# The RWKV scan of a hybrid diffusion backbone: its small products on 64-row tiles, without zero-padded operands

## The chip, the cores and the metric

One core of a Trainium2 chip runs the whole forward pass in one launch. The metric is device time in microseconds, the median of several runs. The engines are called as the profile calls them: PE is TensorE's matmuls, PEld its weight loads, DVE VectorE, ACT ScalarE, POOL GpSimd, SP SyncE, which only issues DMAs here.

## The reference: what is computed

Two layers over 256 context and 256 latent tokens of width 1024. The even layer mixes tokens by retention and grouped-query attention and has a dense SwiGLU; the odd one mixes by differential attention and a bidirectional RWKV-7 scan and has eight experts, of which each token takes two. Only the scan, in the odd layer's mixer, is touched here. It has 8 heads of 64 features and, per head and direction, a 64 x 64 state:

```
def step(s, inp):
    rt, wt, kt, vt, at, bt = inp
    s_new = (s * wt[:, :, None, :]
             + jnp.einsum('bhvk,bhk->bhv', s, at)[..., None] * bt[:, :, None, :]
             + vt[..., None] * kt[:, :, None, :])
    y = jnp.einsum('bhvk,bhk->bhv', s if read_before else s_new, rt)
    return s_new, y
...
for d in range(2):
    f = (lambda t: t[:, ::-1]) if d else (lambda t: t)
    yc, state = rwkv_scan(*[f(t) for t in ctx_dirs[d]], zero, read_before=bool(d))
    yl, _ = rwkv_scan(*[f(t) for t in lat_dirs[d]], state, read_before=bool(d))
```

The context's tokens are scanned first, only for their state; the latent tokens' outputs `y` of both directions are added, normalized per head, scaled and gated, and multiplied with the output projection together with the attention's result.

## The kernel before

The scan runs in chunks of 64 tokens: a half (half 0 is the context, half 1 the latent tokens) has four chunks, and both directions `d` walk them, one upwards, one downwards. Features lie on partitions, two heads to a group of 128: head `2 p + h` has partitions `64 h` to `64 h + 63` of group `p`. `prep` leaves per direction and half the decayed operands `AR` (a and r) and `BK` (b and k), and the chunk decay `WC`. Inside a chunk a unit triangular system is solved; its inverses come ahead of the scan from `inv_blocks` (32 x 32 blocks by TensorE), `inv_diag` (forward substitution, columns shared by VectorE, `tmv`, and GpSimd, `tmg`, both updating `N`) and `inv_join` (`X`, transposed by VectorE, then products `gp` and `wp`), and are stored in `XF`.

`step` handles one chunk of one direction, in four parts between yields:

- the operands: `lm` = products of `BK` with the a and r columns, masked on VectorE into `Lm` (L1128); `bkt` and the lower half of `UV` by transposes (L1132, L1139);
- `z` = `Lm` x `UV` (L1149) plus, from the second chunk on, a x the state `St` (L1152), copied to `zs` (L1158);
- `u` = the inverse `XF` x `zs` (L1162), copied into the upper half of `UV` by ScalarE and VectorE (L1164, L1165);
- `s` = `bkt` x `UV` (L1172), which with `St` and `WC` gives the next state (L1179, L1180); in half 1 also the outputs `Y` (L1187, L1189).

Products of one head have only 64 rows, but are done over all 128 partitions here: the head's operand stands in a buffer whose other 64 partitions are zero. `pad` (four buffers, a and r) and `zpad` (two, for `z`) are cleared by GpSimd once per chain (L1103); their halves are copied in by VectorE and ScalarE (L1118, L1158).

```
pd = pad[cnt[0] % 4]
for h in range(2):
    hs = slice(64 * h, 64 * h + 64)
    (S.copy if h else V.tensor_copy)(pd[hs, :, h, 0:w], ar[hs, :, c])
```

`chain(half)` sends both directions through their steps and prepares the next chunk's operands behind `z`. `chain(0)` is emitted side by side with the second half's `inv_diag` and `inv_join`, `chain(1)` with `finish`, which prepares the gate (`G1`, `G2`) and weights (`whi`, `wlo`) of the output projection. `Y` has two PSUM banks, one per block of 128 tokens. Behind the scan each block is normalized, transposed (L478) and multiplied (`mms`, L267 to L269); `moe_open` lets SP send the experts' weights (L1411), whose buffers take the scan's place in memory.

The code says what depends on what; the order of the instructions on each engine is set by the framework's scheduler when the kernel is built, and stays so, on SP's queue of DMAs too. An fp32 product shows as two records in the profile.

## Time and profile before

| | |
|---|---|
| Time, median of 3 runs | 2155.31 us (2152.7 to 2157.81) |
| Profiled execution, span | 2153.4 us; the page gives no other time of it |
| Busy: PE, PEld | 2045.5 us (95%), 1635.4 us (76%) |
| Busy: DVE, ACT, POOL | 1663.8 (77%), 1220.2 (57%), 166.0 us (8%) |
| DMA | 493.99 MB, mean 229 GB/s |
| Granted TensorE clock, mean | 0.976 |

Busy shares are means over stages with different limits. The page's picture of the span in 40 slices, each 53.8 us, shows this: the DMA engines are busy nine tenths from slice 22 on, where the experts' weights stream in, and nearly idle in slices 17 to 20, where the scan runs. In a row the array's tile stands as rows x columns (128\*64), and a record's duration is longer than the distance to the next record's start, since matmuls are pipelined; distances between starts tell the rate.

### The profile page before, as it was taken

The page shows a single profiled execution, that of the slowest core. Times are in us where ns is not written, and L with a number is a line of the kernel's source. Part 1 is how long each engine was busy: PE and PEld are TensorE (multiplying, and loading weights), DVE is VectorE, ACT ScalarE, POOL GpSimd, SP SyncE. Part 2 cuts the span into 40 slices and gives each one's busy share as a digit, 9 for nine tenths or more (in the row PEclk, how much of TensorE's full clock was granted, in tenths as well). Part 3 has the DMA queues.
Part 4 walks back from the last instruction along what each step waited for, and adds up shares of the span by engine and source line. Part 5 has one row for each costly group of instructions (what it writes and reads, how often), then busy time and mean ns, then how long its engine had stood idle before and what let it go on. Part 6 is the DMA issues. An engine that isn't in the chain of part 4 may idle for free. (4 is left out here: it accounts for less than half of the span.)

```text
span 2153.4 us, 30029 instructions
## 1 busy us (share of the span) xinstructions
PE 2045.5 (95%) x11521; PEld 1635.4 (76%) x11522; DVE 1663.8 (77%) x2099; ACT 1220.2 (57%) x1581; POOL 166.0 (8%) x223
## 2 busy tenths in 40 slices
PE   6999989999999999858999999999999999999997
PEld 2767778777887766748887888888888787888875
DVE  3977783674557556688568999889989999899987
ACT  3543342222235445633337777777777777777775
POOL 0211110000000110284001000000000000000000
PEclk8999999999999999969999999999999999999999
DMA  8435351475645331101077999999999999999993
GB/s 297 160 109 168 110 172 55 152 244 187 203 150 166 111 88 45 36 16 51 21 268 258 366 317 350 332 347 367 355 343 352 350 372 347 339 352 357 366 353 144
DMA packets 224202, 493.99 MB, mean 229 GB/s; under 512 B 11355, under 2 KB 45262, under 8 KB 224054
## 3 DMA queue, kind: packets, MB, share of 16 engines
q1 hardware_dynamic: 219968, 482.62, 64.4%
q10 hardware_dynamic: 4086, 9.40, 1.3%
q8 instruction: 92, 1.51, 0.3%
q14 instruction: 56, 0.46, 0.1%
HBM read 490.87 MB, written 1.11 MB: 228 GB/s over the span
## 5 line engine op out<-in xcount | busy, mean ns | idle before, releaser
L273 DVE TENSOR_TENSOR mlo<-mraw,mhi 128x1024 fp32r<-128x1024 f32 x668 | 789.1, 1221 | 79.2 <-ACT mhi L272 62.4
L272 ACT ACTIVATE mhi<-mraw 128x1024 fp32r<-128x1024 f32 x668 | 682.9, 1057 | 104.3 <-PE y L269 49.0
L262 ACT ACTIVATE whi<-raw 128x1024 fp32r<-128x1024 f32 (+1 forms) x150 | 153.0, 1024 | 279.6 <-PE acc L269 109.6
L263 DVE TENSOR_TENSOR wlo<-raw,whi 128x1024 fp32r<-128x1024 f32 (+1 forms) x146 | 175.1, 1203 | 137.8 <-ACT whi L262 137.4
L267 PE MATMUL acc<-hTh,whi 128*128 128x512 f32 (+1 forms) x504 | 190.7, 380 | 0.0
L268 PE MATMUL acc<-hTl,whi 128*128 128x512 f32 (+1 forms) x504 | 186.6, 371 | 0.0
L269 PE MATMUL acc<-hTh,wlo 128*128 128x512 f32 (+1 forms) x504 | 185.6, 369 | 0.0
L268 PE MATMUL g<-mlo,xh 128*128 128x512 f32 x448 | 182.5, 407 | 0.3 <-POOL mlo L1581 0.3
L337 DVE SCALAR_TENSOR_TENSOR part<-mraw,cond,part 128x1024 f32<-128x1024 f32 x112 | 147.8, 1341 | 40.3 <-DMA mraw<-in_mod_w 40.2
L267 PE MATMUL g<-mhi,xh 128*128 128x512 f32 x448 | 178.6, 399 | 0.0
L267 PE MATMUL u<-mhi,xh 128*128 128x512 f32 x448 | 177.3, 396 | 0.0
L268 PE MATMUL u<-mlo,xh 128*128 128x512 f32 x448 | 177.3, 396 | 0.0
L269 PE MATMUL u<-mhi,xl 128*128 128x512 f32 x448 | 177.1, 395 | 0.0
L269 PE MATMUL g<-mhi,xl 128*128 128x512 f32 x448 | 177.1, 395 | 0.0
L268 PE MATMUL y<-mlo,acts 128*128 128x512 f32 x448 | 175.7, 392 | 0.3 <-DVE mlo L273 0.3
L269 PE MATMUL y<-mhi,acts 128*128 128x512 f32 x448 | 174.8, 390 | 0.0
L267 PE MATMUL y<-mhi,acts 128*128 128x512 f32 x448 | 151.4, 390 | 0.0
L267 PE MATMUL acc<-whi,hTh 128*128 128x512 f32 x336 | 137.7, 413 | 5.3 <-ACT whi L262 3.4
L268 PE MATMUL acc<-wlo,hTh 128*128 128x512 f32 x336 | 135.8, 404 | 4.5 <-DVE wlo L263 4.5
L269 PE MATMUL acc<-whi,hTl 128*128 128x512 f32 x336 | 134.7, 402 | 0.0
L267 PEld LDWEIGHTS acc<-hTh,whi 128*128 128x128 f32 x504 | 95.3, 190 | 22.4 <-issue 4.1
L268 PEld LDWEIGHTS acc<-hTl,whi 128*128 128x128 f32 x504 | 95.0, 189 | 17.6 <-issue 2.8
(437 smaller groups left out, 3510.1 us busy)
## 6 DMA issues: line engine op xcount, KB each, us to landing
mraw<-in_moe_w_gate SPq DMA_DIRECT2D x112, 1024.0 KB
mraw<-in_moe_w_up SPq DMA_DIRECT2D x112, 1024.0 KB
mraw<-in_moe_w_down SPq DMA_DIRECT2D x110, 1024.0 KB
mraw<-in_mod_w SPq DMA_DIRECT2D x96, 512.0 KB
raw<-in_ffn_w_down SPq DMA_DIRECT2D x32, 512.0 KB
raw<-in_odd_w_in SPq DMA_DIRECT2D x26, 512.0 KB
raw<-in_even_w_in SPq DMA_DIRECT2D x24, 512.0 KB
raw<-in_ffn_w_gate SPq DMA_DIRECT2D x20, 512.0 KB
```

The source lines that it names most:

```text
L262: S.activation(h, v, AF.Copy)
L263: (eng or V).tensor_tensor(l, v, h, op=ALU.subtract)
L267: T.matmul(out, ah, bh, start=first, stop=False)
L268: T.matmul(out, ah, bl, start=False, stop=False)
L269: T.matmul(out, al, bh, start=False, stop=last)
L272: S.activation(hi, src, AF.Copy)
L273: eng.tensor_tensor(lo, src, hi, op=ALU.subtract)
L337: V.scalar_tensor_tensor(part[r], w, c_, part[r], op0=ALU.mult, op1=ALU.add)
```

## The change

The zero-padded buffers, their clearing and their copies are gone. Products of one head take the 64 partitions they need, on a 64-row tile of the array (`tile_position=(64 * h, ...)`), and loops go over the heads so that neighbours have different parity `h`. `lm`, `u` and `Y` have a PSUM bank per parity; `Y`'s banks no longer stand for blocks of tokens, so the normalization goes by parity too, and the transposes wait for both. Masked evictions of `Lm` in half 0 are two of half the size. `zs` is one copy, VectorE's for one direction and ScalarE's for the other. The steps of a chain are emitted in a new order: `z` of both directions, operands of the next chunk for direction 0, `u` of both, operands for direction 1, `s` of both, then all outputs.

```diff
-        pad, zpad = [], []
         def chain_pool():
-            e, q = top_pool("chain")
-            pad[:] = [q.tile([128, 4, 2, 128], F32, name=f"pad{i}") for i in range(4)]
-            zpad[:] = [q.tile([128, 4, 2, 64], F32, name=f"zpad{i}") for i in range(2)]
-            for t in pad + zpad:
-                G.memset(t, 0.0)
-            return e, q
+            return top_pool("chain")
+        heads = [(p, h, slice(64 * h, 64 * h + 64)) for p in range(4) for h in range(2)]
...
+        def prepare(d, half, c):
+            a = [acc("lm") for h in range(2)]
+            for p, h, hs in heads:
+                T.matmul(a[h][:, p * w:(p + 1) * w], bk[hs, p, c].rearrange("p a t -> p (a t)"), ar[hs, p, c, 0:w],
+                         start=True, stop=True, tile_position=(64 * h, 0))
             for h in range(2):
-                hs = slice(64 * h, 64 * h + 64)
-                (S.copy if h else V.tensor_copy)(pd[hs, :, h, 0:w], ar[hs, :, c])
...
+                V.tensor_tensor(Lm[:, 4 * h:4 * h + 4, 0:w], a[h][:, 0:4 * w].rearrange("p (a t) -> p a t", a=4),
+                                rc(f"rmask{d}")[:, None, 0:w].to_broadcast([128, 4, w]), op=ALU.mult)
...
+        def state_in(d):
+            for p, h, hs in heads:
+                hd = 2 * p + h
+                T.matmul(zv[hs, p], Lm[:, 4 * h + p, 0:64], UV[:, hd * 64:hd * 64 + 64], start=(p == 0),
+                         stop=(S0 is None and p == 3), tile_position=(0, 64 * h), skip_group_check=True)
+            if S0 is not None:
+                for p, h, hs in heads:
+                    T.matmul(zv[hs, p], ar[hs, p, c, 0:64], S0[hs, p], start=False, stop=(p == 3),
+                             tile_position=(64 * h, 64 * h), skip_group_check=True)
+            zs[d] = q.tile([128, 4, 64], F32, name="zs", tag="zs", bufs=2)
+            (S.copy if d else V.tensor_copy)(zs[d], zv)
+
+        def solve(d, half):
+            u = [acc("u") for h in range(2)]
+            for p, h, hs in heads:
+                T.matmul(u[h][0:64, p * 64:p * 64 + 64], XF[half][hs, d, c, p], zs[d][hs, p],
+                         start=True, stop=True, tile_position=(64 * h, 0))
...
+        def state_out(d, half):
+            for p, h, hs in heads:
+                hd = slice((2 * p + h) * 64, (2 * p + h) * 64 + 64)
+                T.matmul(sv_[hs, p], bkt[:, hd], UV[:, hd], start=True, stop=True, tile_position=(0, 64 * h))
...
+        def outputs(was, states, i):
+            for part in range(2):
+                for p, h, hs in heads:
+                    for d in range(2):
+                        o_, at_ = 64 * (c % 2), (c // 2) * 256 + p * 64
+                        dst = Y[h][o_:o_ + 64, at_:at_ + 64]
+                        if part == 0:
+                            T.matmul(dst, Lm[:, 4 * h + p, 64:128], UV[:, hd], start=(i == 0 and p == 0), stop=False,
+                                     tile_position=(0, o_), skip_group_check=True)
+                        else:
+                            T.matmul(dst, ar[hs, p, c, 64:128], states[d][hs, p], start=False,
+                                     stop=(i == 3 and p == 3), tile_position=(64 * h, o_), skip_group_check=True)
...
         def chain(half):
+            for i in range(4):
+                for d in range(2):
+                    state_in(d)
+                yield
...
+                ahead(0)
+                for d in range(2):
+                    solve(d, half)
+                yield
+                ahead(1)
+                for d in range(2):
+                    state_out(d, half)
+                yield
+                if half:
+                    outputs(was, states, i)
...
-            V.tensor_tensor(yc, yc, G1[:, b], op=ALU.mult)
-            V.tensor_tensor(yc, yc, G2[:, b], op=ALU.add)
-            split_to(mh[:, 4:8, b * 128:b * 128 + 128], ml[:, 4:8, b * 128:b * 128 + 128], tr4(yc))
+            V.tensor_tensor(ycb, ycb, parity(G1, h), op=ALU.mult)
+            V.tensor_tensor(parity(yf, h), ycb, parity(G2, h), op=ALU.add)
+        for b in range(2):
+            split_to(mh[:, 4:8, b * 128:b * 128 + 128], ml[:, 4:8, b * 128:b * 128 + 128], tr4(yf[:, b]))
```

How the instructions move, in three places. First TensorE in the second chain, where a step's `z` ends and the next step's operands begin (numbers behind names tell buffers and PSUM tiles apart); before:

```order
L1149 MATMUL z_8712<-UV_8685,Lm_8669 64x64
L1152 MATMUL z_8712<-St_8426,pad1_8628 64x64
L1126 MATMUL lm_8734<-pad2_8629,BK01_6852 128x256 x2
L1126 MATMUL lm_8738<-pad2_8629,BK01_6852 128x256 x2
L1132 MATMUL tp_8742<-cst_all_64,BK01_6852 128x128 x4
L1139 MATMUL tp_8751<-cst_all_64,vT_5386 128x128 x4
```

and in the changed kernel:

```order
L1137 MATMUL z_8713<-UV_8677,Lm_8657 64x64 x8
L1141 MATMUL z_8713<-St_8442,AR01_6851 64x64 x8
L1137 MATMUL z_8732<-UV_8705,Lm_8685 64x64 x8
L1141 MATMUL z_8732<-St_8454,AR11_6854 64x64 x8
L1244 MATMUL tp_8751<-cst_all_64,vT_5386 128x128 x4
L1111 MATMUL lm_8760<-AR01_6851,BK01_6852 128x128
L1111 MATMUL lm_8761<-AR01_6851,BK01_6852 128x128
```

The two kinds of `z` products, which took turns, now stand in eights; `lm` has twice as many products, of 128 columns and not 256, which alternate between two banks.

Then VectorE at the start of the scan, with the last columns of the first inversion (`tmv`, `N`); before:

```order
L1037 TENSOR_TENSOR tmv<-M,N 128x14
L1039 TENSOR_TENSOR N<-N,tmv 128x7x2
L1118 COPY pad_7760<-AR_6334 64x4x64
L1037 TENSOR_TENSOR tmv<-M,N 128x12
L1039 TENSOR_TENSOR N<-N,tmv 128x6x2
```

and in the changed kernel:

```order
L1037 TENSOR_TENSOR tmv_7345<-M_7064,N_7084 128x14
L1114 TENSOR_TENSOR Lm_7788<-lm_7790,cst_rwkv_5376 128x4x64
L1039 TENSOR_TENSOR N_7084<-N_7084,tmv_7345 128x7x2
L1114 TENSOR_TENSOR Lm_7847<-lm_7848,cst_rwkv_5376 128x4x64
L1037 TENSOR_TENSOR tmv_7351<-M_7064,N_7084 128x12
```

The pad copies are gone from between the columns (five stood before the transposes `X`), and five half evictions of `Lm` stand there, where one whole one stood.

Last VectorE behind the scan, where `yc` is the normalized output (G1 and G2 scale, gate and shift it); before, up to the first block's split into `mixl`:

```order
L1276 TENSOR_TENSOR yc_9367<-yc_9367,G2_8600 128x512
L1274 TENSOR_TENSOR yc_9390<-yc_9390,yrs_9396 128x512
L263 TENSOR_TENSOR wlo_9474<-raw_8610,whi_9473 128x1024
L273 TENSOR_TENSOR mixl_8598<-tp_9380,mixh_8597 128x4x128
L1275 TENSOR_TENSOR yc_9390<-yc_9390,G1_8599 128x512
```

and in the changed kernel, up to both blocks' splits:

```order
L1282 TENSOR_TENSOR yc_9424<-yc_9424,yrs_9430 128x512
L1283 TENSOR_TENSOR yc_9424<-yc_9424,G1_8627 128x512
L1284 TENSOR_TENSOR yf_9404<-yc_9424,G2_8628 128x8x64
L263 TENSOR_TENSOR wlo_9547<-raw_8642,whi_9546 128x1024
L273 TENSOR_TENSOR mixl_8626<-tp_9437,mixh_8625 128x4x128
L273 TENSOR_TENSOR mixl_8626<-tp_9444,mixh_8625 128x4x128
```

The splits now stand behind both sequences. On TensorE 48 products of the output projection stand between the scan and these transposes; before, 37 stood ahead of the first block's and 52 ahead of the second's. GpSimd's queue loses the pads' memsets (6 per chain) and is otherwise in its old order, SP's queue is unchanged.

## Rows read from the trace of the kernel before

**Rows 1.** Stages: us, busy time of each engine (x instructions), granted clock, DMA share, GB/s
```profile
961.70:1007.50 45.80, 42.66 (x774) 39.55 (x773) 39.35 (x105) 17.42 (x37) 21.36 (x52) 0.95 0.07 20
1007.50:1029.70 22.20, 17.68 (x359) 15.08 (x357) 18.55 (x26) 9.97 (x18) 8.15 (x10) 0.77 0.37 120
1029.70:1091.90 62.20, 62.11 (x886) 57.06 (x885) 29.95 (x60) 18.72 (x38) 2.97 (x4) 1.00 0.06 17
1200.00:2000.00 800.00, 800.00 (x3602) 648.80 (x3601) 720.24 (x690) 611.31 (x658) 0.00 (x0) 1.00 0.97 350
```
**Rows 2.** Time line at the scan's end, SP's queue: start, us, engine, line, op
```profile
1090.99 1.38 SPq L1411 DMA_DIRECT2D mraw<-in_moe_w_gate  x1
```
**Rows 3.** Time line at the scan's start; in brackets the idle time before, and its releaser
```profile
953.00 3.62 POOL L1103 MEMSET pad<- 128x1024 f32 x4
953.99 4.18 DVE L1118 COPY pad<-AR 64x256 f32<-64x256 f32 x1 [3.97 <-POOL pad L1103]
...
961.73 2.11 DVE L1048 STREAM_TRANSPOSE X<-N 128x1024 f32<-128x1024 f32 x1
```
**Rows 4.** VectorE by line, 970 to 1007.5 us: busy us, mean ns | idle before
```profile
L1128 DVE TENSOR_TENSOR Lm<-lm,cst_rwkv 128x512 f32<-128x512 f32 x7 | 4.8, 687 | 0.6 <-PE lm L1126 0.5
L1158 DVE COPY zpad<-z 64x256 f32<-64x256 f32 x7 | 2.9, 416 | 3.2 <-PE z L1152 3.1
...
L1118 DVE COPY pad<-AR 64x256 f32<-64x256 f32 x3 | 1.1, 367 | 0.3 <-PE z L1152 0.3
```
**Rows 5.** Time line of TensorE in the second chain, products on one tile after another
```profile
1056.24 0.60 PE L1139 MATMUL tp<-cst_all,vT 128*128 128x128 f32 x4
...
1059.44 0.28 PE L1187 MATMUL Y<-UV,Lm 128*64 128x64 f32 x2
1059.56 0.28 PE L1189 MATMUL Y<-St,pad 128*64 128x64 f32 x2
```
**Rows 6.** The same time line where two column tiles take turns
```profile
1061.19 0.22 PE L1172 MATMUL s<-UV,bkt 128*64 128x64 f32 x1
...
1061.19 0.22 PE L1189 MATMUL Y<-St,pad 128*64 128x64 f32 x1
...
1061.25 0.22 PE L1172 MATMUL s<-UV,bkt 128*64 128x64 f32 x1
```
**Rows 7.** Block products on 64-row tiles: the window's clock, then their time line
```profile
935.00:940.00 5.00, 2.91 (x166) 2.91 (x170) 5.00 (x8) 0.00 (x0) 4.77 (x4) 0.50 0.02 3
...
938.73 0.24 PE L1011 MATMUL off<-AR,BK 64*32 64x32 f32 x1
...
938.83 0.32 PE L1008 MATMUL dg<-AR,BK 64*32 64x32 f32 x6
```
**Rows 8.** Time line between the chains: transposes, pads and the first copy of z
```profile
1007.50 2.10 DVE L1048 STREAM_TRANSPOSE X<-N 128x1024 f32<-128x1024 f32 x1
...
1014.28 4.47 POOL L1103 MEMSET pad<- 128x1024 f32 x4 [20.02 <-PE s L1172]
...
1021.69 2.08 DVE L1118 COPY pad<-AR 64x512 f32<-64x512 f32 x4
...
1031.72 0.41 DVE L1158 COPY zpad<-z 64x256 f32<-64x256 f32 x1 [1.29 <-PE z L1152]
```
**Rows 9.** TensorE by line in the second chain, 1029.7 to 1091.9 us
```profile
L1187 PE MATMUL Y<-UV,Lm 128*64 128x64 f32 x128 | 15.5, 224 | 0.0
```
**Rows 10.** Time line of TensorE where `z` on 128\*64 tiles is followed by `lm`
```profile
1051.16 0.28 PE L1152 MATMUL z<-St,pad 128*64 128x64 f32 x2
1051.38 1.99 PE L1126 MATMUL lm<-pad,BK 128*128 128x256 f32 x8
```
**Rows 11.** Time line behind the scan: the two blocks' transposes, and VectorE before the second
```profile
1100.58 0.62 PE L478 MATMUL tp<-cst_all,yc 128*128 128x128 f32 x4
...
1104.51 0.68 DVE L1276 TENSOR_TENSOR yc<-yc,G 128x512 f32<-128x512 f32 x1
...
1106.66 0.60 PE L478 MATMUL tp<-cst_all,yc 128*128 128x128 f32 x4
```

More of the change, by code (lines that the diff above doesn't have):

```diff
@@ L1110, in step @@
[L1110 removed]
+        St, Y, ops, zs = {}, {}, {}, {}
+        heads = [(p, h, slice(64 * h, 64 * h + 64)) for p in range(4) for h in range(2)]
+        def prepare(d, half, c):
             bk, ar = BK[d, half], AR[d, half]
[L1112 to L1129 removed]
@@ L1145, in step @@
             zv = z[:, 0:256].rearrange("p (a v) -> p a v", a=4)
-            for h in range(2):
-                for p in range(4):
-                    hd = 2 * p + h
-                    T.matmul(zv[64 * h:64 * h + 64, p], Lm[:, hd, 0:64], UV[:, hd * 64:hd * 64 + 64],
-                             start=True, stop=S0 is None, tile_position=(0, 64 * h))
-                    if S0 is not None:
-                        T.matmul(zv[64 * h:64 * h + 64, p], pd[:, p, h, 0:64], S0[:, p],
-                                 start=False, stop=True, tile_position=(0, 64 * h))
@@ L1154, in step @@
-            zs = zpad[cnt[1] % 2]
-            cnt[1] += 1
-            for h in range(2):
-                hs = slice(64 * h, 64 * h + 64)
-                (S.copy if h else V.tensor_copy)(zs[hs, :, h], zv[hs])
-            yield
-            u = acc("u")
-            for hd in range(8):
-                T.matmul(u[0:64, hd * 64:hd * 64 + 64], XF[half][:, d, c, hd // 2], zs[:, hd // 2, hd % 2],
-                         start=True, stop=True, tile_position=(0, 0))
-            S.copy(UV[0:64, 0:256], u[0:64, 0:256])
@@ L1167, in step @@
+        def state_out(d, half):
+            c, ar, Lm, bkt, UV = ops[d]
+            S0 = St.get(d)
             s = acc("s")
             sv_ = s[:, 0:256].rearrange("p (a v) -> p a v", a=4)
[L1169 to L1173 removed]
+            for p, h, hs in heads:
+                hd = slice((2 * p + h) * 64, (2 * p + h) * 64 + 64)
+                T.matmul(sv_[hs, p], bkt[:, hd], UV[:, hd], start=True, stop=True, tile_position=(0, 64 * h))
@@ L1180, in step @@
                 V.tensor_tensor(Sn, Sn, wc, op=ALU.mult)
-            if half:
-                b, o_ = c // 2, 64 * (c % 2)
-                first = (o_, b) not in seen
-                for hd in range(8):
-                    p, h = hd // 2, hd % 2
-                    last = (o_, b) in seen and hd == 7
-                    T.matmul(Y[b][o_:o_ + 64, hd * 64:hd * 64 + 64], Lm[:, hd, 64:128], UV[:, hd * 64:hd * 64 + 64],
-                             start=(first and hd == 0), stop=False, tile_position=(0, o_), skip_group_check=True)
-                    T.matmul(Y[b][o_:o_ + 64, hd * 64:hd * 64 + 64], pd[:, p, h, 64:128], S0[:, p],
-                             start=False, stop=last, tile_position=(0, o_), skip_group_check=True)
-                seen.add((o_, b))
@@ L1195, in chain, with ahead @@
         def chain(half):
-            gens = [[step(d, half, i if d == 0 else 3 - i) for d in range(2)] for i in range(4)]
-            for g in gens[0]:
-                next(g)
+            at_ = lambda d, i: i if d == 0 else 3 - i
+            for d in range(2):
+                prepare(d, half, at_(d, 0))
             for i in range(4):
-                live = list(gens[i])
-                first_ = True
-                while live:
-                    for g in list(live):
-                        if next(g, 1) == 1:
-                            live.remove(g)
-                    if first_ and i < 3:
-                        for g in gens[i + 1]:
-                            next(g)
-                        first_ = False
-                    yield
+                for d in range(2):
+                    state_in(d)
+                yield
+                was, states = dict(ops), dict(St)
+                nxt = {}
+                def ahead(d):
+                    if i < 3:
+                        prepare(d, half, at_(d, i + 1))
+                        nxt[d] = ops[d]
+                        ops[d] = was[d]
+                ahead(0)
[3 more added lines that the diff above has]
+                ahead(1)
+                for d in range(2):
+                    state_out(d, half)
+                yield
+                if half:
+                    outputs(was, states, i)
+                ops.update(nxt)
+                yield
@@ L1254, in layer1 @@
         banks(acc=range(4), y=(4, 5))
-        for b in range(2):
-            Y[b] = ybank("Y")
+        for h in range(2):
+            Y[h] = ybank("Y")
         weave((chain(1), 16), (finish(), 10))
@@ L1262, in layer1 @@
         cur["xn"] = 2
-        for b in range(2):
-            y = Y[b]
-            yv = y.rearrange("p (h w) -> p h w", h=8)
+        yf = yp.tile([128, 2, 512], F32, name="yf")
+        parity = lambda x, h: x.rearrange("q b (p h w) -> q b p h w", p=4, h=2)[:, :, :, h]
+        for h in range(2):
+            yv = Y[h].rearrange("p (g w) -> p g w", g=8)
             m = st.tile([128, 8], F32, name="ym")
```

39 lines of the change are left out of this document (11 added, 28 removed).

## The prediction

> **What bounds the kernel now.** I read the stage table first, then the time line of the handover to the experts, then the scan's stretches by line, then single matmuls. The stage table [rows 1] shows the experts' stage, from 1200 us on, with the DMA engines at 0.97 and 350 GB/s and TensorE busy throughout: it runs at its own pace, whatever came before. Its stream of weights starts only when the scan's last products are issued: SP sends the first megabyte at 1090.99 us [rows 2]. So what the scan loses or gains moves the end of the kernel one for one, unless the few steps between scan and experts change too. The scan itself has three stretches that differ.
>
> In the last one, 1029.7 to 1091.9 us (the second half's chain, `chain(1)`), TensorE is busy 62.11 of 62.20 us at full clock, VectorE only 29.95 [rows 1]: TensorE's stream of small products is the bound. In the first, VectorE is: it idles 3.97 us for a copy into `pad0`, which waits for GpSimd's memsets of the pads (from 953.00, 3.62 us), and then that copy takes 4.18 us [rows 3] where its like take 0.37 [rows 4], so that the transposes of the block inverses start at 961.73 [rows 3]. Between them the first half's chain shares VectorE with the inversion of the second half's blocks (39.35 of 45.80 us busy [rows 1]).
>
> **The price of a small product.** An fp32 product is two records in this trace. Eight records of `Y`, four each of two products that alternate on one tile, start 0.06 us apart: the pairs stand at 1059.44 and 1059.56 [rows 5], so 58 ns a record. Where the order happens to put `Y` and `s` records of different column tiles side by side, two start together: both at 1061.19, the next at 1061.25 [rows 6]: half the price, 29 ns. On 64-row tiles the records of the block products (32 columns at the granted clock of 0.50, that is 1.2 GHz: half the columns at half the clock, so 58 ns each if alone) come six in 0.32 us where one lasts 0.24: (0.32 - 0.24) / 5 = 16 ns [rows 7]. So different tiles do work side by side, also row tiles, and the bounds for a 64-column record are 16 ns (four tiles in flight) and 58 ns (none). I take 29 ns, two tiles in flight, as the rows of the same size show it [rows 6].
>
> **The change, part by part.** All gains are against the profiled span of 2153.4 us.
>
> *A. Start of the scan.* The pads' memsets and copies go. The stop on VectorE, 3.97 + 4.18 = 8.1 us [rows 3], goes with them. Added before the transposes: five half evictions of `Lm` instead of one whole (0.69 [rows 4]); a half has 256 columns, and a copy of 256 columns takes 0.42 [rows 4], so +1.4 us, while four more pad copies of 0.37 [rows 4] go, -1.5. The products they evict now stand behind transposes at the slow clock; I put 2 us for that. GpSimd ended its own part of the inversion at 953.0, ahead of the new point. Gain 8.1 - 2 = 6 us.
>
> *B. First chain beside the inversion.* On VectorE, 970 to 1007.5 us: seven whole evictions (4.8 us) become eleven halves (4.6), seven half copies of `z` (2.9) become four whole ones (the other direction's are ScalarE's; 1.7), the pad copies (1.1) go [rows 4]: 2.5 us. Its 3.1 us of waiting for `z` I leave as it is. Gain 2.5.
>
> *C. Join and start of the second chain.* Before, from the first transpose at 1007.50 to the first copy of `z` at 1031.72 there are 24.2 us. GpSimd's second set of memsets (from 1014.28, 4.47 us) and the pad copies (1021.69, 2.08 us) stand ahead of the first `lm` product [rows 8]. Without pads these products run during the join, so at VectorE's 14.2 us mark it evicts four `Lm` (4 x 0.69) and does one weight split, about 4 us, less 1 us of pad and `z` copies inside the join: 17.5 us. Gain 6.7. The clock is at 0.77 in this stretch [rows 1]; I assume the same after.
>
> *D. Second chain.* 64-column records: `z` 256, `u` 128, `s` 128, `Y` 256 (two groups of 128, one of them in [rows 9]), 768 in all, from 58 to 29 ns: 44.2 us become 22.1. `lm`: 48 records of 256 columns at (1.99 - 0.39) / 7 = 0.23 us [rows 10], 11 us, become 96 of 128 columns on two row tiles; one alone is priced by the transposes of 128 columns, (0.60 - 0.27) / 3 = 0.11 [rows 5], two in flight 0.057: 5.5 us. Together -27.6. Against it: some records overlap already (the prices above, with 48 transposes and `finish`'s share of about 4 us, add up to 65 us in a 62.2 us window), 3 us; the order now changes the array's tiling some 24 times more, and a change costs 1051.38 - 1051.22 - 0.06 = 0.10 us [rows 10], 2.4 us; and with the work halved the chain `St` to `z` to `u` to `UV` to `s` shows in places, above all in the last step, where nothing is prepared for a next one, 2 us. VectorE's 29.95 us stay under the 42 that are left. Gain 27.6 - 7.4, about 20 us.
>
> *E. Behind the scan.* The output now needs both head parities before its transposes. Before, the first block's transposes stood behind 37 products of the output projection, at 1100.58, 8.7 us behind the chain, and the second's at 1106.66 [rows 11]. Now 48 products, at 8.7 / 37 = 0.235 us 11.3 us, stand ahead of both, and both wait for VectorE's two sequences, which ended near 1105.2, some 14 us behind. TensorE waits about 3 us, where it waited 1.5 before. Loss 1.5 us. ScalarE's table load and the weight loads on SP keep their places; SP's first load now waits for the first chain's `Lm` and not for a pad, and is freed long before its split.
>
> Sum: -6 - 2.5 - 6.7 - 20 + 1.5 = -33.7, a span of 2119.7 us. The page gives no time beside the span; the median of the runs, 2155.3, is 1.9 us more, which I add: **2121.5 us**.
>
> **A rule to weigh.** The rows show `Y` and `s` records, both over all 128 rows and on different column tiles, starting together [rows 6], and I price by that. The Trainium skill, TensorE: Matmul & The Clock Gate, section "The mechanism", says that a weight load overlaps matmuls in flight only where the row group differs. By that, neighbours that differ in columns alone would gain nothing, which is the first rival below and its 2132.5 us; the trace speaks against it in the one place it shows.
>
> **The rivals.**
> 1. *Column neighbours don't overlap.* The `Lm` half of `z`, `s` and the first half of `Y` (64 products each, 384 records) lie over all 128 rows and keep 29 ns more each, 11 us: 2132.5. Against it: [rows 6]. For it: there only a few records in a row do so.
> 2. *Row tiles don't overlap either*, or the doubled weight loads of `lm` take the gain. D is then nothing (768 x 58 ns stay, `lm` too, the tiling changes come on top, and the overlap already there covers them): -6 - 2.5 - 6.7 + 1.5 = -13.7, 2141.5. Against it: [rows 7].
> 3. *More than two tiles in flight* in `Y` and deeper interleaving (16 ns): 768 x 13 ns = 10 us more, until VectorE's 30 us and the chain's waits stop it; I allow 8: 2113.5.
> 4. *The clock falls* in the second chain, because TensorE, its work halved, waits between steps. The mean is 0.77 in the join [rows 1], and 0.50 where TensorE worked 2.91 of 5 us [rows 7]. The 42 us of work left would take 84 at 1.2 GHz, +42, so -33.7 + 42 = +8: 2163, slower. It turns to a loss once four fifths of that work run at the low level (33.7 / 42). Against it: at the low level the work itself would fill TensorE, and the window behind the join, which TensorE fills, has 1.00 [rows 1].
> 5. *The change does not do what it says*: in the first chain the scheduler puts the `lm` products of one parity together, four on one row tile. That stretch is VectorE's, so the time stays 2121.5 and it has no chance of its own; in the second chain they alternate.
>
> **How the numbers follow.** Forecast 0.60, rival 1 0.10, rival 2 0.13, rival 3 0.12, rival 4 0.05. A measurement of this kernel tells about 0.2%, 4.3 us, from no change. Of rival 4 part of the way lands within that. So faster 0.95, same 0.03, slower 0.02. The forecast's own range is 2113 to 2131 (A to C may each miss by 3 us, D by 5). The range for 8 in 10 goes from 2110 to 2142: it takes in the rivals 1 to 3 up to their own times and leaves rival 4 and the far ends out.
>
> **What would show it.** The transposes of the first inverses near 955 us, those of the second near 999; the first copy of `z` of the second chain near 1016; the first load of expert weights near 1055; in the second chain `z`, `u`, `s` and `Y` records 29 ns apart and the granted clock at 1.00; TensorE's wait behind 48 output products. A chain that still lasts 60 us would prove D wrong, a first load at 1055 with an end past 2130 the one-for-one carry, a granted clock under 0.9 there would be rival 4.

## The result, and the profile after

The changed kernel takes 2131.68 us (median of 4 runs, 2128.83 to 2133.62), the kernel before in runs beside it 2154.52: a ratio of 0.9889, 95% interval 0.9875 to 0.9903. Its profiled execution is 2132.66 us with a span of 2130.9, which is 22.5 less than before's span. The forecast was 2121.5 and a gain of 33.7: the direction and the main mechanism held, and a third of the gain did not come.

The first view is the table of stretches of the changed kernel (busy time of each engine with its instructions, granted clock, DMA share, GB/s), cut at the points that the prediction named:

```profile
948.00:957.70 9.70, 9.70 (x41) 8.03 (x41) 4.60 (x24) 2.46 (x5) 5.59 (x16) 0.50 0.27 84
957.70:1005.10 47.40, 46.61 (x811) 40.99 (x813) 35.03 (x103) 13.79 (x27) 20.99 (x52) 0.71 0.04 13
1005.10:1025.20 20.10, 18.66 (x404) 16.39 (x402) 14.24 (x23) 8.43 (x14) 1.92 (x4) 0.66 0.42 134
1025.20:1067.30 42.10, 41.64 (x901) 35.40 (x899) 25.32 (x50) 13.94 (x28) 1.97 (x4) 1.00 0.07 26
```

The second chain is 42.1 us long where it was 60.3, TensorE still fills it, and its clock is 1.00: that is the gain. But the first chain's stretch is as long as before, and its clock column reads 0.71 where before's read 0.95 [rows 1]; the join reads 0.66 where it was 0.77.

Next VectorE's time line of the changed kernel, with the idle time before an instruction and its releaser in brackets:

```profile
942.28 2.02 DVE L1018 STREAM_TRANSPOSE M<-Lc 128x1024 f32<-128x1024 f32 x1
...
952.39 0.42 DVE L1114 TENSOR_TENSOR Lm<-lm,cst_rwkv 128x256 f32<-128x256 f32 x1 [2.19 <-PE lm L1111]
...
956.57 0.42 DVE L1114 TENSOR_TENSOR Lm<-lm,cst_rwkv 128x256 f32<-128x256 f32 x1 [2.26 <-PE lm L1111]
...
957.76 2.06 DVE L1048 STREAM_TRANSPOSE X<-N 128x1024 f32<-128x1024 f32 x1
...
971.09 0.42 DVE L1114 TENSOR_TENSOR Lm<-lm,cst_rwkv 128x256 f32<-128x256 f32 x1 [4.80 <-PE lm L1111]
...
1005.10 2.05 DVE L1048 STREAM_TRANSPOSE X<-N 128x1024 f32<-128x1024 f32 x1
...
1018.86 1.29 DVE L1114 TENSOR_TENSOR Lm<-lm,cst_rwkv 128x512 f32<-128x512 f32 x2 [2.76 <-PE lm L1111]
...
1022.55 1.29 DVE L1114 TENSOR_TENSOR Lm<-lm,cst_rwkv 128x512 f32<-128x512 f32 x2 [2.41 <-PE lm L1111]
...
1025.15 0.42 DVE L1144 COPY zs<-z 128x256 f32<-128x256 f32 x1 [0.17 <-PE z L1141]
...
1067.31 1.29 DVE L1274 TENSOR_REDUCE ym<-Y 128x8 f32<-128x512 f32 x2 [0.51 <-PE Y L1186]
```

The same time line of the kernel before gives the two ends that were not shown yet:

```profile
942.38 2.02 DVE L1018 STREAM_TRANSPOSE M<-Lc 128x1024 f32<-128x1024 f32 x1
...
1091.99 1.29 DVE L1267 TENSOR_REDUCE ym<-Y 128x8 f32<-128x512 f32 x2 [0.80 <-PE Y L1189]
```

With these and [rows 3, 8] the span falls into five stretches, and each term of the sum into one of them (us):

| stretch | before | after | measured | predicted |
|---|---|---|---|---|
| transpose of `M` to the first transposes of `X` | 19.35 | 15.48 | -3.9 | A -6 |
| to the second transposes of `X` | 45.77 | 47.34 | +1.6 | B -2.5 |
| to the first copy of `z` of the second chain | 24.22 | 20.05 | -4.2 | C -6.7 |
| to the first reduction of `Y` | 60.27 | 42.16 | -18.1 | D -20 |
| to the end of the span | 1061.41 | 1063.59 | +2.2 | E +1.5 |

The bracketed waits point to one cause for A, B and C. VectorE's waits, grouped by who waited for whom (total, times, longest), from 940 us to the first copy of `z`; the first fence is the changed kernel, the second the kernel before:

```profile
DVE Lm L1114 <- PE lm L1111: 18.0, 8, 4.8
```
```profile
DVE Lm L1128 <- PE lm L1126: 3.6, 6, 1.0
```

VectorE now waits 18.0 us for `lm`, where it waited 3.6. TensorE was not idle meanwhile: in the rows above it is busy all of 948 to 957.7 us at 0.50, the 1.2 GHz level. In the kernel before, where it began later, it was at full clock from some 962.5 us on, but for a dip to 0.60 in 976 to 980 us, behind 3 us without work. Two explanations fit these rows: TensorE is late because it is slow (theory C, the clock), or because `lm` waits in its queue for something else, such as the bank that `off` holds (theory P, the place). The experiments start there.

### The profile page after: what moved, and what is told of

The parts are those of the page before. It is cut to its first block, busy times and chain, and to the rows that moved or that the text cites. A ratio compares the mean times of both kernels' runs of the same rounds, so it can differ in the third digit from the quotient of the medians.

```text
span 2130.9 us, 30220 instructions
## 1 busy us (share of the span) xinstructions
PE 2038.5 (96%) x11649; PEld 1621.1 (76%) x11650; DVE 1646.4 (77%) x2083; ACT 1210.4 (57%) x1557; POOL 152.6 (7%) x211
## 5 line engine op out<-in xcount | busy, mean ns | idle before, releaser
L267 PEld LDWEIGHTS acc<-hTh,whi 128*128 128x128 f32 x504 | 95.4, 190 | 22.5 <-issue 4.1
```

Of the source, the lines that this page charges most:

```text
L267: T.matmul(out, ah, bh, start=first, stop=False)
```

## The experiments

All times of stretches come from the profiled executions, one of each kernel. The kernels e1 to e9 are described below the table. Its columns are: transposes of `M` to first `X`; first to second `X`; second `X` to first copy of `z`; from there to the reduction of `Y`; the granted clock from 956 to 976 us; median time and ratio to before.

| kernel | M-X | X-X | X-z | z-Y | clock | time, ratio (95%) |
|---|---|---|---|---|---|---|
| before | 19.35 | 45.77 | 24.22 | 60.27 | mostly 1.00 | 2154.5 |
| changed | 15.48 | 47.34 | 20.05 | 42.16 | 0.50 | 2131.7, 0.9889 (0.9875 to 0.9903) |
| e1 same tile | 15.53 | 53.58 | 22.99 | 51.94 | 0.50 | 2148.9, 0.9981 (0.9971 to 0.9992) |
| e2 two Lo | 17.67 | 42.51 | 20.19 | 42.16 | 0.50 | 2130.0, 0.9895 (0.9881 to 0.9909) |
| e3 before, alternating | 19.36 | 41.78 | 23.49 | 54.26 | mostly 1.00 | 2143.3, 0.9957 (0.9941 to 0.9972) |
| e4 dense start | 10.68 | 40.20 | 23.44 | 42.17 | 1.00, from 968 us lower | 2126.8, 0.9875 (0.9853 to 0.9898) |
| e5 + late loads | 10.87 | 48.00 | 21.09 | 42.17 | 0.50 | 2121.8, 0.9842 (0.9828 to 0.9856) |
| e6 grouped z | 15.48 | 47.36 | 20.24 | 40.53 | 0.50 | 2130.9, 0.9890 (0.9874 to 0.9906) |
| e7 all three | 10.66 | 39.36 | 20.49 | 41.44 | 1.00, from 968 us lower | 2121.1, 0.9841 (0.9827 to 0.9855) |
| e8 + last step | 10.86 | 47.02 | 20.48 | 40.22 | 0.50 | 2121.8, 0.9832 (0.9810 to 0.9854) |
| e9 + dense join | 10.87 | 39.27 | 21.36 | 39.33 | 1.00, from 968 us lower | 2119.7, 0.9833 (0.9818 to 0.9849) |

**Does the overlap of neighbours make D?** The heads in another order, so that neighbours share a tile:

```
-heads = [(p, h, slice(64 * h, 64 * h + 64)) for p in range(4) for h in range(2)]
+heads = [(p, h, slice(64 * h, 64 * h + 64)) for h in range(2) for p in range(4)]
```

> The changed kernel with the heads taken in another order: first the four of one parity, then the four of the other, so that neighbours lie on the same tile. Tiles, operands, banks and evictions stay. Theory (the gain of the second chain is the overlap of neighbours on different tiles): of its 64-column records the 512 of z, u and s go from about 29 back to 58 ns (+14.8 us), the 128 records of the second part of Y from 15 to 29 ns (+1.8), the 96 records of lm from 59 to about 112 ns (+5.1). From the first copy of z to the first reduction of Y it takes 42.2 + 21.7, about 62 to 64 us, as before the change, and the whole kernel loses 22 to 30 us (the join and the first chain lose a little too): 2154 to 2162. Rival (the gain comes from what is no longer computed or copied: zeros, pads, two evictions instead of one): the stretch stays within 3 us of 42.2 and the time within 5 us of 2131.7.

The second chain takes 51.94 us and the kernel 17 us more than the changed kernel (less than the 22 expected). TensorE's time line of this kernel in the second chain, start and length of a run of records; the last four lines are a place where `z` ends on one tile and `u` begins on another:

```profile
1035.85 0.96 PE L1141 MATMUL z<-St,AR 64*64 64x64 f32 x16
...
1037.33 1.71 PE L1111 MATMUL lm<-AR,BK 64*128 64x128 f32 x16
...
1039.99 1.54 PE L1150 MATMUL u<-zs,XF 64*64 64x64 f32 x32
...
1082.12 0.22 PE L1141 MATMUL z<-St,AR 64*64 64x64 f32 x1
1082.17 0.22 PE L1150 MATMUL u<-zs,XF 64*64 64x64 f32 x1
1082.18 0.22 PE L1141 MATMUL z<-St,AR 64*64 64x64 f32 x1
1082.23 0.22 PE L1150 MATMUL u<-zs,XF 64*64 64x64 f32 x1
```

and that of the changed kernel:

```profile
1025.64 0.68 PE L1141 MATMUL z<-St,AR 64*64 64x64 f32 x16
1026.26 0.66 PE L1244 MATMUL tp<-cst_all,vT 128*128 128x128 f32 x4
1026.84 1.16 PE L1111 MATMUL lm<-AR,BK 64*128 64x128 f32 x16
...
1036.04 0.69 PE L1186 MATMUL Y<-St,AR 64*64 64x64 f32 x32
```

A lone 64-column record lasts 0.22 us by itself, so sixteen of `z` in 0.68 start (0.68 - 0.22) / 15 = 31 ns apart on alternating tiles, and (0.96 - 0.22) / 15 = 49 ns in this order. `lm`, with 0.28 for the last, goes from 59 to 95 ns. The 49 ns are a mean, not the pace of one tile: in the last four lines the records of each tile start 0.06 us apart, like the 58 ns of the kernel before, though these products have 64 rows, and the two tiles run side by side. Eight records on one tile are followed by eight on the other, and at each such border the last of one run beside the first of the next. That is one reason why the expectation was 10 to 12 us too high: it put 58 ns between all of them.

The new order of the heads costs 9.8 of the 18.1 us of D. The other 8.3 do not come without alternation, because this edit leaves one in place: the outputs `Y` of the two directions lie on different column tiles and still take turns, record by record. TensorE's busy time with `Y` (then its records, clock, DMA share and GB/s) in the kernel before, in e1 and in the changed kernel:

```profile
1020.00:1095.00 75.00, 16.44 (x256) 0.95 0.11 32
1020.00:1095.00 75.00, 8.63 (x256) 0.93 0.24 78
1020.00:1095.00 75.00, 6.96 (x256) 0.98 0.41 144
```

`Y` alone is 7.8 us shorter in e1 than before. So nearly all of D is tiles taking turns, about half of it by heads and most of the rest by directions; leaving out the zeros saves TensorE little by itself in this chain, since 64 rows cost the same 58 ns on one tile as 128. The stretch is not near 42.2, so the rival falls. The records that lie on four tiles, Y's state part, run (0.69 - 0.22) / 31 = 15 ns apart: the prediction's rival 3 is right for that half of `Y`.

**Columns alone.** The kernel before, with only the order of `z` and `s` changed, operands still padded:

```
-for h in range(2):
-    for p in range(4):
+for p in range(4):
+    for h in range(2):
...
-            T.matmul(zv[64 * h:64 * h + 64, p], pd[:, p, h, 0:64], S0[:, p],
+    for h in range(2):
+        if S0 is not None:
+            T.matmul(zv[64 * h:64 * h + 64, p], pd[:, p, h, 0:64], S0[:, p],
```

> The kernel before with one part of the change alone: in z and in s neighbours lie on different column tiles (the four of one pair of heads are Lm h0, Lm h1, St h0, St h1). The zero-padded operands, the 128-row products of u and lm, Y's order, the memsets and all copies stay. Theory (column neighbours overlap): 256 records of z and 128 of s in the second chain go from 58 to 29 ns, 384 x 29 = 11 us, so the stretch from the first copy of z to the first reduction of Y goes from 60.3 to about 49 us and the kernel to about 2143.5, while the transposes of X stay at 961.7 and within 2 us of 1007.5. Rival (neighbours that differ in columns alone do not overlap, and the gain in the changed kernel is that of the row tiles): the stretch stays within 2 us of 60.3, and the time is 2152 to 2156.

```profile
1038.92 0.34 PE L1149 MATMUL z<-UV,Lm 128*64 128x64 f32 x4
1039.08 0.29 PE L1153 MATMUL z<-St,pad 128*64 128x64 f32 x4
1039.20 0.29 PE L1149 MATMUL z<-UV,Lm 128*64 128x64 f32 x4
```

Four records start every 0.117 us, 29 ns apiece, though all lie over 128 rows and differ in columns alone. The time is as expected, 2143.3, but not by the expected way: the second chain gives 6.0 us and not 11, and the first chain gives 4.0 us, where two were allowed. In the second chain TensorE is busy with `z` for 7.30 us where it was 11.62, and with `s` for 6.08 where it was 7.54: before, the borders between tiles had overlapped already, and part of `s` had lain beside `Y` [rows 6]. The rival falls. The Trainium skill, TensorE: Matmul & The Clock Gate, section "The mechanism", has weight loads overlap only where the row group differs. By that these records would have stayed at 58 ns; the 29 ns measured decide against it.

**Why are A, B and C short? The bank.** Two buffers for `Lo`, so that `off`'s bank is free earlier:

```
-Lo = qI.tile([128, 16, 32], F32, name="Lo", tag="Lo", bufs=1)
+Lo = qI.tile([128, 16, 32], F32, name="Lo", tag="Lo", bufs=2)
```

> The changed kernel with two buffers instead of one for Lo, so that the bank of the off-diagonal products of the second half is freed before the first half's join and the other parity's lm of the first step need not wait for it. Theory P (the first chain is late because that bank is held): VectorE's wait of 4.80 us for lm before 971.09 us goes, the second transposes of X start near 1000.5 instead of 1005.1, and the kernel gains 4 to 5 us: 2127. Theory C (it is late because TensorE, busy without a gap from 948 to 982 us, works at a granted clock of 0.50): the lm come in another order, but the same work stands ahead, the granted clock stays at 0.50 till about 980, and the second transposes start within 2 us of 1005.1: 2130 to 2133.

The clock stays at 0.50 till 984 us, as theory C had it; but the second transposes start at 1002.22, and counted from the transposes of `M` they gain 2.6 us (1.63 + 1.55 + 0.79 + 1.69 us of waits stand ahead of the first transposes, which lose 2.2, and the wait of 4.80 is gone). The time, 0.9895, is not different from the changed kernel's 0.9889. So the truth lies between the two theories: the bank costs a part of B, since without its wait the stretch between the transposes is 4.8 us shorter, and nearly half of that is lost again in the start.

**The clock.** The first four transposes of the first chain, four times over:

```
 t = tpp()
-for p in range(4):
+for p in [p for _ in range(4 if (half, d, c) == (0, 0, 0) else 1) for p in range(4)]:
     T.transpose(t[:, p * 128:(p + 1) * 128], bk[:, p, c].rearrange("p a t -> p (a t)"), ident)
```

> The changed kernel with the first four transposes of the first chain (BK of direction 0) made four times over, so that 20 transposes of 128 rows and 128 columns follow one another at 948.5 us instead of 8. Twelve of them are of no use and cost 12 x 0.27 = 3.2 us at the low clock. Theory C (the first chain is late because TensorE works at the low clock): the granted clock rises to 1.00 near 953 instead of 984, the first transposes of X start up to 3 us later (961), but VectorE's waits for lm behind them (4.80, 1.24, 2.00 and 1.13 us) shrink to under half, and the second transposes of X start near 1001 instead of 1005.1: 2127 to 2130. Theory P (what is late is held by a bank or by VectorE, not by TensorE's speed): whatever the clock does, both transposes of X start 2 to 3 us later than in the changed kernel, and the time is 2133 to 2135.

VectorE's time line and the stretches of this kernel:

```profile
955.28 2.11 DVE L1048 STREAM_TRANSPOSE X<-N 128x1024 f32<-128x1024 f32 x1
...
995.48 2.08 DVE L1048 STREAM_TRANSPOSE X<-N 128x1024 f32<-128x1024 f32 x1
```
```profile
952.00:956.00 4.00, 4.00 (x22) 3.71 (x21) 3.48 (x17) 1.19 (x2) 3.45 (x11) 0.63 0.48 150
956.00:960.00 4.00, 4.00 (x88) 3.56 (x87) 3.99 (x5) 2.38 (x4) 3.47 (x10) 1.00 0.00 0
```

The clock rises near 955 us, and both transposes of `X` come early: the second one 9.6 us before the changed kernel's, though some 3 us of useless work stand ahead of it and the run reached the scan 2.3 us later. The longest wait for `lm` before the join is 0.20 us. Theory P falls for the stretch as a whole.

Two things are mixed in this, the clock and the order, which the scheduler changed too. The next kernel, e5, has the same order as e4 on TensorE, VectorE and ScalarE up to the output projection, and in its profiled execution the clock did not rise before 980 us:

```profile
952.00:956.00 4.00, 4.00 (x17) 3.41 (x16) 3.89 (x3) 1.82 (x4) 3.71 (x10) 0.50 0.00 0
956.00:960.00 4.00, 4.00 (x74) 3.49 (x75) 3.89 (x11) 1.19 (x2) 3.36 (x9) 0.50 0.00 0
...
980.00:984.00 4.00, 4.00 (x84) 3.61 (x81) 3.14 (x10) 0.37 (x1) 0.52 (x1) 0.88 0.02 4
```
```profile
952.28 2.10 DVE L1050 STREAM_TRANSPOSE X<-N 128x1024 f32<-128x1024 f32 x1
...
966.46 0.43 DVE L1116 TENSOR_TENSOR Lm<-lm,cst_rwkv 128x256 f32<-128x256 f32 x1 [6.09 <-PE lm L1113]
...
1000.28 2.08 DVE L1050 STREAM_TRANSPOSE X<-N 128x1024 f32<-128x1024 f32 x1
```

So the order is worth 4.6 to 4.8 us up to the first transposes, with either clock (M-X 10.7 to 10.9 in all five kernels with the dense start): only three half evictions of `Lm` are left ahead of the transposes, and none waits, where the changed kernel has five and two of them wait 4.45 us. And the clock is worth 7.7 to 7.8 us from the first to the second transposes, by two pairs with the same order there: 40.20 against 48.00 us (e4, e5) and 39.36 against 47.02 (e7, e8). The two profiles without the rise had reached the scan 2.7 to 5 us earlier (`M` at 939.61 and 941.41 against 944.07 to 944.60), so the net loss in those two is smaller than 8 us. Only one execution of each kernel has a trace. In e8, two of the five executions took 2113.8 and 2114.3 us at a mean clock of 0.979 and 0.981, the other three 2121.8 to 2123.5 us at 0.974 to 0.976: that fits a clock that rises early in some executions of one kernel and not in others, but where it rose in those two no trace shows. In the changed kernel's order, the low clock held from 948 to past 980 us in all three profiles (changed, e6, and e1 with its other head order), so what that order would take at full clock no trace shows.

**The loads, and the pause in the join.** With the start mended, the join is late: e4 takes 23.44 us there. TensorE's time line of e4, where the first run of records ends near 1006:

```profile
1004.36 1.67 PE L1072 MATMUL wp<-X,Gs 32*32 32x32 f32 x98
1010.40 1.05 PE L1072 MATMUL wp<-X,Gs 32*32 32x32 f32 x30 [4.38 <-issue]
```

"issue" means that TensorE waited for nothing that the trace shows. The late loads:

```
+        if after is not None:
+            G.tensor_copy(raw[:, 0:1], after)
...
-raws = [wload(..., 2, 512) for n, c in order]
+raws = [wload(..., 2, 512, after=XF[1][:, 0, 0, 0, 0:1] if 2 <= i < 7 else None) for i, (n, c) in enumerate(order)]
```

> The kernel of the dense start (the first four transposes four times over), and beside it five of the eight loads of odd_w_out wait for the last write of XF[1] (a copy of one column per load on GpSimd), so that they no longer run while TensorE does the second join. In the dense start TensorE stood still for 4.38 us in the middle of wp (till 1010.40 us) with no wait that the trace shows, while the DMA engines were at 0.96. Theory L (TensorE waits there for its own instructions, which come by a DMA queue and stand behind the weights): the pause falls under 1 us, the granted clock stays higher in the join, the first copy of z of the second chain goes from 1018.9 to about 1014, the span from 2125.0 to 2119 to 2121. Rival (the pause belongs to the place in TensorE's program, or to its operands, whatever the DMA engines do): it stays over 3.5 us, and the time within 2 us of the dense start's.

The pause is gone and the time is 0.9842 against 0.9875 for e4, but the profile does not decide for theory L: the clock was low, so TensorE came to this place slowly, and the first copy of `z` is at 1021.37, not 1014. In e7, with the clock up, the pause is 2.10 us. The column that the loads wait for is written by VectorE, and is not XF[1]'s last write as the expectation has it, so e7's loads still ran beside `wp` (DMA engines at 0.94 in 1004 to 1008 us). The last kernels put that right, and change the last step too:

```
-after=XF[1][:, 0, 0, 0, 0:1]
+after=XF[1][:, 0, 0, 0, 32:33]
...
-            for part in range(2):
+            for part in ((1, 0) if i == 3 else (0, 1)):
...
-                for d in range(2):
+                for d in range(0 if half and i == 3 else 2):
                     state_out(d, half)
```

> The three changes together (dense start, late loads, grouped z), with two more. (a) The late loads of odd_w_out wait for a column of XF[1] that ScalarE writes behind wp, where they had waited for one that VectorE writes ahead of it (in the kernel with all three they began at 1003 us, and TensorE's pause in wp was still 2.10 us). (b) The last step of the second chain computes no new state, which nobody reads (32 records of s, four VectorE operations), and does Y's state part ahead of its Lm part, so that it lies in the wait for the copies of u. Theory for (a): the pause in wp falls under 0.5 us, although the clock is at 1.00 there, and the first copy of z comes about 2 us earlier against the first transposes of X than the 59.9 us of the kernel with all three. Rival: it stays near 2 us. Theory for (b): from the first copy of z to the first reduction of Y 40.5 instead of 41.4 us, and the first load of expert weights comes up to 1.5 us earlier against that reduction, since the space it waits for is freed by the Lm part of Y and the copies of u. Together 3 to 5 us below the kernel with all three: a span of 2114 to 2117, if the granted clock rises in the start as it did there.

```profile
1006.72 1.61 PE L1074 MATMUL wp<-X,Gs 32*32 32x32 f32 x95
1010.28 1.11 PE L1074 MATMUL wp<-X,Gs 32*32 32x32 f32 x33 [1.95 <-issue]
```
```profile
1008.00:1012.00 4.00, 2.05 (x60) 1.87 (x55) 1.04 (x1) 0.57 (x1) 0.00 (x0) 0.70 0.01 4
```

With the DMA engines at 0.01 in 1008 to 1012 us the pause is still 1.95 us. So (a) falls: the weights are not its cause, at most what made e4's longer. In the kernels of the new form it stands 83 to 114 of 128 records into `wp`, and it is short where TensorE comes to that place slowly (0 in e5, 0.38 in the changed kernel). What fixes its place is a count. Work of TensorE (matmuls, then weight loads, with their numbers) and of the other engines from the start of the span to within the pause, in e8, in e9 (twelve more transposes, described below) and in the kernel before:

```profile
0.00:1009.50 1009.50, 936.76 (x5932) 727.39 (x5933) 676.55 (x1079) 399.69 (x647) 137.46 (x200) 0.96 0.42 133
0.00:1007.60 1007.60, 932.99 (x5932) 723.21 (x5933) 676.87 (x1079) 400.11 (x648) 138.27 (x200) 0.97 0.42 133
0.00:1017.20 1017.20, 932.29 (x5805) 725.59 (x5806) 682.81 (x1079) 404.00 (x659) 145.31 (x206) 0.96 0.42 132
```

In all kernels of the new form that pause, TensorE stops behind matmul 5931 or 5932. In e9 that is 83 records into `wp` and in e8 95: the twelve extra transposes ahead move it by twelve. In the kernel before, whose `wp` also pauses (0.47 us), it stops behind matmul 5805, 127 matmuls and as many weight loads earlier. So the pause belongs to a place in TensorE's list of instructions, not to `wp`, its operands or the weights. That TensorE there runs ahead of its own supply of instructions, which would come in blocks of about that size, fits this; the supply itself no trace shows.

Of (b), the chain took 40.2 us for 41.4, as expected (40.5), but the first load of expert weights that waits for the scan's end came later, not earlier (6.4 us behind the reduction of `Y`, 1.0 in e7): SP's order changed as well, and a load of odd_w_out that waits for a split now stands ahead of it. The expected span of 2114 to 2117 us was meant for a clock that rises in the start. The profiled execution, where it did not, has 2120.1; the two short executions named above have 2112.0 and 2112.5.

**The price of a change of tiling.** `z` with both directions' `Lm` parts first:

```
-                for d in range(2):
-                    state_in(d)
+                state_in()
```

> The changed kernel with z's products in another order: first the Lm part of both directions (128 rows, column tiles), then the state part of both (64 x 64 tiles), where the changed kernel does one direction after the other. Two changes of the array's tiling fall away in each step. Price of one by the trace of the changed kernel: 16 records of z at 0.029 us are 0.46, and the next kind starts 0.61 us behind, so about 0.14 us. Theory (a change of tiling costs that): the four groups of z take 2.45 - 0.28 = about 2.2 us a step, the second chain 41 instead of 42.2 us, the time about 2130.5. Rival (the 0.14 us belong to each new group of products, not to the tiling, or the later copy of direction 0 is waited for): z's four groups keep 2.45 us or TensorE waits for zs, the chain stays at 42 us or more, the time within 1 us of 2131.7 or above.

```profile
1035.98 1.15 PE L1137 MATMUL z<-UV,Lm 128*64 128x64 f32 x32
1037.06 1.15 PE L1143 MATMUL z<-St,AR 64*64 64x64 f32 x32
1038.14 1.16 PE L1111 MATMUL lm<-AR,BK 64*128 64x128 f32 x16
```

Thirty-two records take 1.08 us where two times sixteen took 0.61 + 0.61: each change that falls away saves 0.14 us, eight of them 1.1 us. The chain is 40.53 us, 1.6 less, of which 0.2 us have moved into the join. The theory holds in the trace; the time (0.9890) can't tell it from the changed kernel. The Trainium skill, TensorEngine Tiling (Array Packing), section "Tiling Modes", says that a change of mode drains the engine and gives no price; the trace fits that, with 0.14 us.

**Together, and the join's clock.** e7 has the dense start, the late loads and the grouped `z`:

> The dense start, the late loads and the grouped z together. If the three gains are of different places, they add up: the dense start 6, the late loads 4 to 6, the grouped z 1: a span of 2118 to 2120 us where the changed kernel has 2130.9. If the grouped z or the late loads bring nothing, 2120 to 2125.

Its span is 2119.4 us and its median 2121.1: in the expected range. Against e4 the join is 2.95 us shorter, with a pause 2.28 us shorter; the late loads had been put at 4 to 6 us. e9 adds to e8 twelve useless transposes ahead of the second `gp`:

```
-gp = acc("gp")
+gp = acc("gp"); [T.transpose(gp[:, 0:128], ident, ident) for _ in range(12 * half)]
```

> The kernel with the last step changed, with twelve more useless transposes of 128 x 128 into the bank of gp, ahead of the second gp. They cost 12 x 0.11 = 1.3 us at the high clock, part of it in TensorE's wait for UV. In all kernels so far the granted clock falls to 0.50 within some 5 us of the second transposes of X and rises again only behind lm and the transposes of the second chain. Theory (the join is late because of the clock): it stays at 1.00 through gp, wp and lm, which at the low clock take about twice as long, and from the second transposes of X to the first copy of z it takes 17 instead of 20.5 us. Rival (VectorE's transposes and copies of XF, some 8 us, and ScalarE's copies of gp and wp set the pace of the join, TensorE's speed does not): 20 us or more, and the time within 1 us of the kernel without them or up to 1.3 us above.

The rival fits better, but the test is only half of what was meant. It took 21.36 us from the second transposes to the first copy of `z`, although the clock was 0.85 and 0.73 around the transposes and 1.00 in 1004 to 1008 us. But it fell again, to 0.63 in 1008 to 1012 us, where sixteen records of `lm` took 2.08 us, as in the changed kernel, and not the 1.16 of full clock. In the kernels of the new form the join takes 20 to 21.4 us (23.4 in e4 with the long pause, 23.0 in e1 with its order of heads), whichever part of it ran at full clock. In it stands a row of steps on VectorE and ScalarE, the copies of XF up to 1004.5 us in e9, ScalarE's copies of `gp` and `wp`, and `lm` behind `wp` in TensorE's order. What a join at full clock throughout would take no run shows.

e5, e7, e8 and e9 beat both kernels: their intervals lie under the changed kernel's. Among the four they overlap, so about 0.984 of before is what can be said of each. e4 alone can't be told from the changed kernel by time.

## Why the prediction was right, and where it was short

*D, the second chain: right.* 18.1 of 20 us. The price of 29 ns held (29 to 31), for column neighbours too, so rival 1 is out, and row tiles overlap, so rival 2 is out. So did the 58 ns of a record on one tile, with 64 rows too. The change of tiling was 0.14 us, not 0.10; `lm` ran at 59 ns a record, not 57, with its own changes on top (96 records in 6 runs of 1.09 us, 6.5 us for 5.5). e1 shows that tiles taking turns make the gain. The total came out better than its terms: TensorE's busy time with `z` fell by only 2.9 us (11.62 to 8.74 in the stretch), where the forecast had 7.4, and that with `Y` by 9.5, where it had 7.4; the 7.4 us taken off for overlap, tiling and waits made up for it. Rival 4 did not come in this chain: its clock is 1.00.

*A, the start: the step that failed is "the products they evict now stand behind transposes at the slow clock; I put 2 us for that".* It is 4.45 us, the two bracketed waits at 952.39 and 956.57. The dense start's order, with three evictions ahead of the transposes instead of five, gets it back at either clock.

*B, the first chain: the step that failed is "its 3.1 us of waiting for `z` I leave as it is".* I had looked at VectorE's own work alone, since it was the bound [rows 4]. Its work in the stretch fell from 39.35 to 35.03 us, more than the 2.5, but it waited: 4.80 us at 971.09, which hung on the bank of `off` (e2), and 4.8 us more up to 986 us for `lm` and `s`. TensorE became the bound, since it works at 1.2 GHz till past 980 us, and the same-parity runs of `lm`, four on one row tile, stand in its queue (rival 5, which I had given no price because the stretch was VectorE's; no run tested that order by itself). The clock was an assumption without a term in this stretch; I had put it only into the second chain (rival 4). With the clock up and the order of the dense start the stretch takes 39.3 to 40.2 us, less than the 43.3 that I had forecast.

*C, the join: the step that failed is "without pads these products run during the join".* Only four of a first group do; the rest stand behind `wp`, and VectorE waits 2.76 and 2.41 us for them at 1018.86 and 1022.55. 4.2 for 6.7 us.

*E, behind the scan: 2.2 for 1.5.* TensorE's wait for `yf` was only 1.47 us, where I had put 3; what I had not priced is SP. Its queue in the changed kernel, and in the kernel before:

```profile
1066.72 0.34 SPq L240 DMA_DIRECT2D sc2b<-mrow  x1
...
1068.30 0.63 SPq L1420 DMA_DIRECT2D mraw<-in_moe_w_gate  x1
```
```profile
1089.60 0.34 SPq L240 DMA_DIRECT2D sc2b<-mrow  x1
```

The load of `sc2b` waits 41.3 us in the changed kernel, for the `Lm` part of `Y`. Before, it was issued 2.39 us ahead of the reduction of `Y`; now it is 0.59 ahead, and the first expert load is 0.99 behind the reduction where it was 1.00 ahead [rows 2]. That load sets the end, as forecast: it came 22.7 us earlier, and the span is 22.5 shorter. This term was read, not tested.

*The total.* 2131.7 us lies 0.7 above the forecast's own range, 2113 to 2131, and within 1 us of rival 1's 2132.5. That nearness is chance, since rival 1 is out; A, B and C miss 8.7 of the 11.2 us, for the clock, the bank and the waits in their order.

## What to carry to other kernels

Price a small product by its neighbour: a 64-column record on one tile took 58 ns with 64 rows as with 128, two tiles in turn ran at 29 to 31 ns a record, rows or columns, and four at 15. So it is not the zeros that cost time here but the tile left idle beside them; order the products so that neighbours alternate, by heads or by directions, and group products of one tiling, at 0.14 us a change. When work is taken off an engine that is not the bound, look at its granted clock in every stretch afterwards: half the pace can hand the bound over to it; here, with the same order, the first chain was 7.7 to 7.8 us longer than at full clock. And where evictions stand ahead of a critical step in an in-order queue, count the wait for each, not only its length.

## What was not expected of the hardware

- TensorE was busy without a gap from 948 to 982 us by the records and kept the 1.2 GHz level throughout; in kernels with the same order on TensorE it rose to full speed near 955 us in some profiles (e4, e7) and only near 980 in others (e5, e8). What decides it was not found.
- On one tile a 64-column record takes 58 ns whether it has 64 or 128 rows (e1, the kernel before). Means of 43 to 50 ns for such runs come from their borders, where two tiles overlap.
- TensorE pauses up to 4.4 us within the 128 records of `wp`, on 32 x 32 tiles, with no wait in the trace, in one kernel with idle DMA engines. It does so behind the same count of its own instructions, 5931 or 5932 matmuls, in every kernel of the new form that pauses, wherever `wp` lies. Why that place holds it up is open.
